# Sum of squared differences by row: another order of the last pieces, and a closing without barriers

## The chip, the cores and the metric

One core of one Trainium2 chip. Times are device microseconds of a whole execution; the span is the stretch that the profile covers, from the first issued load to the last instruction. The program runs on one core, so there is no second die to compare with; all the runs reported here were classed fast, and the granted clock was 1.00 in each. A semaphore is a counter by which one engine waits for another; at a barrier every engine waits for all the others.

## The reference

```python
batch, dim = 1024, 4096            # x and y, float32, standard normal
def reference(x, y, axis):         # axis = -1
    return np.sum((x - y) ** 2, axis=axis).astype(np.float32)
```

33.5 MB are read and 4 KB written.

## The kernel before

Each of the 128 partitions holds 8 rows of 4096 columns side by side, so that a load is a run of columns over all partitions: 32768 columns of x and as many of y. The buffers hold 6 rows; rows 6 and 7 go where rows 0 and 1 lay. VectorE subtracts in place, ScalarE squares and sums each piece of a row into one column, and pieces of one row are added up at the end. A few columns of row 3 ("late") are held back and loaded near the end, so that there is work that needs no new load of x.

```python
xw = [16384, 8192, 3072, 2688, 1312, 768, 352]   # widths of the loads of x
yw = [15648, 8192, 3072, 2688, 1312, 768]        # of y; the first stops 736 short of row 3's end
late, last = 736, 352
...
ys += [(cut, cut + late), (N - last, N)]         # row 3's end, then row 7's last 352 columns
...
for j, (c0, c1) in enumerate(ys):
    final, tail = j == len(ys) - 1, j == len(ys) - 2
    ...
        sub(*piece)                              # VectorE
        if final:                                # row 7: VectorE squares its last piece itself
            nc.vector.wait_ge(acts, squared[row_parts[r][-2]])
            nc.vector.tensor_reduce(out=head, in_=parts_of(r, len(row_parts[r]) - 1), ...)
            ...
            nc.vector.tensor_tensor_reduce(..., scalar=head, accum_out=results[:, r : r + 1])
            continue
        square(*piece, where[piece])             # ScalarE
        if tail:                                 # row 3: ScalarE adds its two parts
            nc.scalar.activation(out=results[:, r : r + 1], in_=b, func=Identity, bias=a)
...
nc.sync.wait_ge(sums, n["sums"])
nc.sync.wait_ge(acts, n["acts"])
nc.sync.dma_start(out=ov, in_=results).then_inc(stored, 16)
nc.sync.wait_ge(stored, 16)
prog.close()                                     # moves all of this ahead of the entry block's branch
```

The work is put into the program's entry block. Behind it come the branch and what leaving the tile context emits: a barrier of all engines, the clearing of the semaphores by GpSimd, a second barrier.

## Time and profile before

| | before |
|---|---|
| time, median of 3 runs | 86.06 us (86.02 to 86.1) |
| profiled run: time, span | 85.87, 84.1 us |
| last load landed | 80.30 |
| store issued | 81.71 |
| store landed | 83.1 |

In a group's line the columns are: source line, engine, operation, output and input, count, busy time and mean, then the idle time of that engine ahead of them and what ended it. In a timeline they are start, duration, engine, line, operation. In a line of an instruction's records come the count, the durations (least, median, greatest, in ns) and when the first and the last started. "Readout" below is the short instruction behind a square that writes out its sum (ACTIVATION_READ_ACCUMULATOR on ScalarE, DVE_READ_ACCUMULATOR2_ANT on VectorE). The lines of the kernel before stand in the prediction.

### The profile page before, as it was taken

What the parts mean: (1) busy time and instruction counts of PE and PEld (TensorE: products, weight loads), DVE (VectorE), ACT (ScalarE), POOL (GpSimd) and SP (SyncE); (2) the same over time, 40 slices, a digit from 0 to 9 for tenths busy, and PEclk for the clock granted to TensorE, in tenths of its full rate; (3) what the DMA queues carried; (4) which work ended last, traced back from release to release, by engine and by line L of the source; (5) the groups of instructions that cost most, each with busy time, mean ns of one, the idle gap of its engine ahead of it and who ended that gap; (6) DMA issues with size and microseconds to landing.
All of it is one profiled execution on the core that took longest, in us unless ns stands there. A gap on an engine that the chain in (4) does not pass through costs nothing.

```text
span 84.1 us, 110 instructions
## 1 busy us (share of the span) xinstructions
DVE 36.3 (43%) x17; ACT 31.6 (38%) x26; POOL 0.2 (0%) x4
## 2 busy tenths in 40 slices
DVE  0000000000000000000899999990699999199870
ACT  4200000000000000000007979799505979997980
POOL 0000000000000000000000000000000000000000
DMA  9479999992999999995899979996999999999900
GB/s 499 187 312 499 499 499 499 499 436 92 447 476 476 476 476 476 476 476 249 358 390 499 499 327 421 499 452 296 438 421 438 424 424 425 400 424 412 363 0 2
DMA packets 2304, 33.56 MB, mean 399 GB/s; under 512 B 384, under 2 KB 640, under 8 KB 1280
## 3 DMA queue, kind: packets, MB, share of 16 engines
q1 hardware_dynamic: 2304, 33.56, 94.1%
HBM read 33.55 MB, written 0.00 MB: 399 GB/s over the span
## 4 chain that ended last, share of the span: by engine, by line
DMA 71%; DVE 14%; ACT 10%; SPq 1%; issue 0%
DMA Y<-in_y_dram 71%; DVE X L172 14%; ACT X L178 10%; SPq L114 1%; ACT results L219 0%
## 5 line engine op out<-in xcount | busy, mean ns | idle before, releaser
L172 DVE TENSOR_TENSOR X<-X,Y 128x4096 f32<-128x4096 f32 (+8 forms) x13 | 35.6, 2781 | 45.2 <-DMA Y<-in_y_dram 45.1
L178 ACT ACTIVATE X<-X 128x4096 f32<-128x4096 f32 (+7 forms) x12 | 29.4, 2449 | 48.7 <-DVE X L172 48.7
L178 ACT ACTIVATION_READ_ACCUMULATOR X<-X 128x1 f32 x12 | 2.2, 186 | 0.0
L178 ACT ACT_TABLE_LOAD x1 | 1.3, 1283 | 1.3 <-PEq L264 1.3
L202 DVE CUSTOM_DVE_ANT_0 Y<-X,head 128x352 f32<-128x352 f32 x1 | 0.6, 583 | 0.1
L219 ACT ACTIVATE results<-parts 128x1 f32<-128x1 f32 x1 | 0.3, 294 | 0.0
L196 DVE TENSOR_REDUCE head<-parts 128x1 f32<-128x3 f32 x1 | 0.1, 150 | 0.0
L235 DVE TENSOR_REDUCE results<-parts 128x1 f32<-128x2 f32 x1 | 0.1, 147 | 0.0
L264 POOL MEMSET const-bfloat16-1.0<- 128x1 bf16 x1 | 0.1, 102 | 0.0
L264 POOL MEMSET const-uint8-127<- 128x1 uint8 x1 | 0.1, 102 | 0.0
L264 POOL MEMSET const-float32-0.0<- 128x1 f32 x1 | 0.1, 99 | 0.2 <-issue 0.2
L264 POOL MEMSET const-float32-1.0<- 128x1 f32 x1 | 0.1, 99 | 0.0
L202 DVE DVE_READ_ACCUMULATOR2_ANT results<- 128x1 f32 x1 | 0.1, 81 | 0.0
## 6 DMA issues: line engine op xcount, KB each, us to landing
Y<-in_y_dram SPq DMA_DIRECT2D x1, 7824.0 KB, 39.8
X<-in_x_dram SPq DMA_DIRECT2D x1, 4096.0 KB, 48.6
Y<-in_y_dram SPq DMA_DIRECT2D x1, 4096.0 KB, 58.0
X<-in_x_dram SPq DMA_DIRECT2D x1, 1536.0 KB, 14.9
Y<-in_y_dram SPq DMA_DIRECT2D x1, 1536.0 KB, 18.2
X<-in_x_dram SPq DMA_DIRECT2D x1, 1344.0 KB, 17.5
Y<-in_y_dram SPq DMA_DIRECT2D x1, 1344.0 KB, 20.4
X<-in_x_dram SPq DMA_DIRECT2D x1, 656.0 KB, 21.5
```

What stands on the lines that cost most here:

```text
L114: nc.sync.dma_start(out=dst[:, home(c0, c1)], in_=src[:, c0:c1]).then_inc(sem, 16)
L172: nc.vector.tensor_sub(out=a, in0=a, in1=Y[:, home(c0, c1)]).then_inc(diffs, 1)
L178: nc.scalar.activation(out=a, in_=a, func=Square, accum_out=acc).then_inc(acts, 1)
L196: nc.vector.tensor_reduce(out=head, in_=parts_of(r, len(row_parts[r]) - 1), axis=mybir.AxisListType.X, op=add).then_inc(sums, 1)
L202: nc.vector.tensor_tensor_reduce(out=Y[:, home(*piece)], in0=X[:, home(*piece)], in1=X[:, home(*piece)], scale=1.0, scalar=head, op0=mult, ...
L219: nc.scalar.activation(out=results[:, r : r + 1], in_=b, func=Identity, bias=a).then_inc(acts, 1)
L235: nc.vector.tensor_reduce(out=results[:, r : r + 1], in_=parts_of(r, len(row_parts[r])), axis=mybir.AxisListType.X, op=add,).then_inc(sums, 1)
L264: nc = _bacc.Bacc("TRN2", target_bir_lowering=False, num_devices=1)
```

## The change

Two things are changed together. The tail: other widths; row 3's end becomes the very last piece and is squared by VectorE, which adds the rest of the row as a scalar operand; row 7 is squared by ScalarE alone and summed by a VectorE reduce behind all else. The Identity on ScalarE and the first reduce go. The closing: the tile context is closed and compiled while it is still empty, so its barriers come at the start; at the end GpSimd alone waits for the store and clears the semaphores.

```diff
+        tc.close()
+        tc.compile()
 ...
+    def close(self, sem, value):
+        self.nc.gpsimd.wait_ge(sem, value)
+        self.nc.clear_and_free_semaphores(self.sems)
 ...
-    xw = [16384, 8192, 3072, 2688, 1312, 768, 352]
-    yw = [15648, 8192, 3072, 2688, 1312, 768]
-    late, last = 736, 352
+    xw = [16384, 8192, 5568, 1824, 512, 288]
+    yw = [16224, 8192, 2656, 2912, 928, 896, 512]
+    late, last = 160, 288
 ...
-    ys += [(cut, cut + late), (N - last, N)]
+    ys += [(N - last, N), (cut, cut + late)]
 ...
             if final:
-                nc.vector.wait_ge(acts, squared[row_parts[r][-2]])
-                nc.vector.tensor_reduce(out=head, ...)
 ...
-                    scalar=head,
+                    scalar=parts_of(r, 1),
 ...
-            if tail:
-                nc.scalar.activation(out=results[:, r : r + 1], in_=b, func=Identity, bias=a)
 ...
+    complete(7)                      # VectorE: wait for ScalarE, reduce row 7's five parts
     nc.sync.wait_ge(sums, n["sums"])
-    nc.sync.wait_ge(acts, n["acts"])
     nc.sync.dma_start(out=ov, in_=results).then_inc(stored, 16)
-    nc.sync.wait_ge(stored, 16)
-    prog.close()
+    prog.close(stored, 16)
```

## The prediction

> **What bounds the kernel now.** I read the page first, then the chain of waits in order of time, then the timeline of the last microseconds, and last the records of the program's closing line.
>
> The page of the kernel before, its head and the two widest groups:
>
> ```profile
> span 84.1 us, 110 instructions
> DVE 36.3 (43%) x17; ACT 31.6 (38%) x26; POOL 0.2 (0%) x4
> HBM read 33.55 MB, written 0.00 MB: 399 GB/s over the span
> DMA 71%; DVE 14%; ACT 10%; SPq 1%; issue 0%
> L172 DVE TENSOR_TENSOR X<-X,Y 128x4096 f32<-128x4096 f32 (+8 forms) x13 | 35.6, 2781 | 45.2 <-DMA Y<-in_y_dram 45.1
> ```
>
> No engine is busy half of the span. VectorE idles 45.2 us, nearly all on loads of y. 33.55 MB in about 80 us is the kernel; what can be saved is what follows the last byte, as the change reads the same bytes. The stretch from 59.65 (y's second load has landed) to 73.47 shows DMA share 1.00 and 420 to 426 GB/s in the view by windows: in steady state one column of one operand (128 x 4 B = 512 B) takes 512 / 426,000 = 1.20 ns.
>
> The chain of waits in order of time, its end:
>
> ```profile
> 53.11 20.36 DMA Y<-in_y_dram
> 73.47 0.02 issue
> 73.49 3.04 DVE X L172 x2
> 76.53 0.02 issue
> 76.56 4.75 ACT X L178 x8
> 81.31 0.02 issue
> 81.33 0.29 ACT results L219
> ```
>
> The last loads arrive one by one (issue plus time to landing, from the DMA list): y up to column 27648 at 66.98, up to 30336 at 73.47, to 31648 at 76.61, to 32416 at 78.49, row 3's 736 columns at 79.37, the last 352 at 61.30 + 19.0 = 80.30. The timeline:
>
> ```profile
> 79.53 0.83 ACT L178 ACTIVATE X<-X 128x768 f32<-128x768 f32 x1
> 80.26 0.19 ACT L178 ACTIVATION_READ_ACCUMULATOR X<-X 128x1 f32 x1
> 80.33 0.53 DVE L172 TENSOR_TENSOR X<-X,Y 128x352 f32<-128x352 f32 x1
> 80.39 0.82 ACT L178 ACTIVATE X<-X 128x736 f32<-128x736 f32 x1
> 80.77 0.15 DVE L196 TENSOR_REDUCE head<-parts 128x1 f32<-128x3 f32 x1
> 81.00 0.58 DVE L202 CUSTOM_DVE_ANT_0 Y<-X,head 128x352 f32<-128x352 f32 x1
> 81.11 0.18 ACT L178 ACTIVATION_READ_ACCUMULATOR X<-X 128x1 f32 x1
> 81.33 0.29 ACT L219 ACTIVATE results<-parts 128x1 f32<-128x1 f32 x1
> 81.52 0.08 DVE L202 DVE_READ_ACCUMULATOR2_ANT results<- 128x1 f32 x1
> 81.71 0.35 SPq L245 DMA_DIRECT2D out_dram<-results  x1
> ```
>
> From the last landing to the store's issue pass 1.41 us. Two paths end together: VectorE at 81.60 (352 columns subtracted, reduced, squared) and ScalarE at 81.62 (736 columns squared, the Identity that adds row 3's halves). The chain names ScalarE, by 0.02 us. The store lands 1.4 us after its issue, at 83.1. What follows, from the records of the closing line:
>
> ```profile
> L278 POOLq EVENT_SEMAPHORE  x4: 17/17/17, 83.4 to 84.0; - x4
> L278 SPq COMPARE_BRANCH  x1: 33/33/33, 83.1 to 83.1; - x1
> L278 POOLq EVENT_SEMAPHORE_RANGE_CLEAR  x1: 138/138/138, 83.7 to 83.7; - x1
> ```
>
> So SyncE wakes at 83.1 and branches; a barrier of all engines forms at 83.5, GpSimd clears all semaphores in one 138 ns instruction at 83.7, a second barrier ends at 84.0. That is nearly 1 us with no work in it.
>
> **What the Trainium skill says.** "ScalarE: Activation LUTs", section "What ACT_TABLE_LOAD costs", gives an ACTIVATE with immediate scale and bias 186 ns + 0.833 ns per column, and about 93 ns more for a pointer operand. The trace agrees: 768 columns took 827 ns (826 by the formula), 4096 took 3617 (3598), and the Identity, with its bias pointer, 294 ns on one column. "VectorE: DVE Perf Modes", section "Mode 2×_2P", has fp32 tensor_tensor held at 1x; the trace's subtractions (527 ns at 352 columns, 4421 at 4096) lie on 161 + 1.04 N. "DMA: Bandwidth & Descriptors", section "Anatomy of one DMA", puts most of a small DMA's fixed 2 us into the wait for the write's receipt; here the 4 KB store took 1.4 us, and the change leaves it. "Runtime: NRT & Kernel Launch", section "The launch sequence", lists work around the kernel that no program removes; here the profiled run measured 85.87 us against a span of 84.1, so 1.8 us lie outside of the span, and I keep them.
>
> **The change, part by part.** First the start. The tile context's own drains and barriers now come before the work. The first two loads still go into the entry block ahead of them, so the DMA starts as before. The other loads wait for perhaps 1 us more of barriers and a branch; but the second load of y occupies the queue until 40.19, so nothing is lost.
>
> The middle. Third load of x: 5568 columns instead of 3072, which needs rows 0 and 1 freed, so it is issued after row 1 is squared (52.74 before, some 53.3 now, as y's first load is 576 columns longer at about 1.05 ns, 0.6 us) instead of at 48.41. y's second load fills the queue to 59.65 + 0.6 = 60.25, so this too is hidden. The load count stays 15.
>
> The tail. All bytes still end at about 80.30. I place the other landings by counting columns of both operands against the before kernel's landings, at 1.20 ns each: y to 30144 ends with column 60128 against 59936 at 73.47, so 73.70; y to 31072: 62880 against 62560 at 76.61, so 76.99; to 31968: 63776 against 64096 at 78.49, so 78.11; to 32480: 64800 against 64832 at 79.37, so 79.33; to 32768: 65376 against 65536 at 80.30, so 80.10; row 3's last 160 at 80.30.
>
> VectorE, by 161 + 1.04 N, successors starting 0.07 before the predecessor's recorded end: 1440 columns from 73.72; 1472 from 75.31 to 77.00; 928 from 77.01 to 78.14; row 6's reduce (0.15) and 896 to 79.34; 512 to 80.05; 288 from 80.12 to 80.58; 160 to 80.84; the square-and-add of 160 (583 - 192 x 1.04 = 383 ns) from 80.92 to 81.30. VectorE alone would be done with row 3 at 81.3.
>
> ScalarE, by 186 + 0.833 N: 1472 can start at 77.03 and takes 1.41; then 928 (0.96), 896 (0.93), 512 (0.61), 288 (0.43). The sum is 4.34 and each operand is ready before its turn, so it runs through to 81.37, and with the accumulator's read (0.09 past the end, as in 81.11 + 0.18 against 80.39 + 0.82) to 81.46. Then VectorE's reduce of row 7's five parts: 0.04 + 0.15, to 81.65; the store's issue 0.09 later, 81.74. Before: 81.71. So the tail gains nothing, by my sum: the Identity (0.29) goes, but row 7 now has all of its pieces on ScalarE, where 352 columns were on VectorE, and a reduce stands behind it. I take 0 with ±0.2.
>
> The end. Store issued at 81.7, landed at 83.1. GpSimd waits for it: about 0.05 to wake, perhaps its drain (0.09) and a gap of 0.1 ahead of the clear as before, 0.14 for the clear: 83.35 to 83.4 against 84.07. One range clear is assumed, as the semaphores are allocated in one go. Gain: 0.7.
>
> Sum: start 0, middle 0, tail 0.0, end -0.7. 86.06 - 0.7 = 85.36; I put 85.3, since the other four engines are long finished when GpSimd ends, which may shorten the runtime's closing a little.
>
> **The rivals.** (1) The tail is worth its full intent: VectorE sets the end, row 7's reduce starts at 81.3, the store at 81.5: 0.2 to 0.3 more, 85.0. For it: VectorE is at rest from 81.3 in my sum. Against: ScalarE's 4.34 us after 77.03. It takes the third y load landing 0.2 us earlier than I counted. (2) The clearing is not on the path, or GpSimd clears 19 semaphores one by one: 19 x 138 ns = 2.6 us, 88 us. Against: before, one range clear did it. (3) The runtime's closing takes the place of the barrier removed: the 0.7 us stay, 86.0. For it: 1.8 us outside of the span, of which the profile shows nothing. Against: before, the engines' barrier came ahead of these, not within. (4) The late issue of the third x load starves the queue at 60. Issues took up to 3.16 us each when many loads were outstanding; a bubble would move the last landing one for one. Against: 53.3 is 7 us ahead of need.
>
> **Range and chances.** Tail ±0.2, end ±0.15, runs ±0.1 (86.02 to 86.1), and the rivals: 84.9 to 85.7. Faster by over 2% means under 84.34, 1 us below my sum, more than rival 1 and a shorter closing can give: 0.05. Slower needs rival 2: 0.01. Within 2%: 0.94.
>
> **What would show it.** The last load should land at 80.3 ± 0.2. ScalarE should run without idle time from the 1472-column square to the 288-column one, and the reduce of five parts should wait for ScalarE, not for VectorE's own square of 160. If it starts right after the latter, the tail step is wrong. Behind the store's landing there should be one range clear on GpSimd and no event semaphores of other engines; the span should end 0.2 to 0.3 us after the landing, at 83.4. If the span shrinks by 0.7 and the time doesn't, rival 3 holds. A gap in the DMA row near 60 us is rival 4.

## The result, and the profile after

| | before | after |
|---|---|---|
| time, median of 4 runs each | 86.04 us | 85.32 us (85.2 to 85.4) |
| ratio, 95% interval | | 0.9916 (0.9899 to 0.9934) |
| profiled run: time, span | 85.87, 84.1 | 85.35, 83.5 |
| last load landed | 80.30 | 65.07 + 15.4 = 80.47 |
| store issued | 81.71 | 81.82 |
| store landed | 83.1 | 83.2 |

A ratio here is the mean time of one kernel's runs over that of the other's of the same rounds, so it is not quite the ratio of the medians beside it. The change saves 0.7 us, under 1%: by the rule of 2% the two count as the same.

The page after, its head:

```profile
span 83.5 us, 109 instructions
DVE 36.3 (44%) x18; ACT 31.7 (38%) x27; POOL 0.2 (0%) x4
HBM read 33.55 MB, written 0.00 MB: 402 GB/s over the span
```

The same bytes, and busy times within 0.1 us. The chain of waits, its end:

```profile
54.11 16.24 DMA Y<-in_y_dram
70.35 0.02 issue
70.37 2.94 DVE X L165
73.31 0.02 issue
73.33 8.28 ACT X L171 x14
81.61 0.02 issue
81.64 0.16 DVE results L178
```

ScalarE's part of the last stretch has grown from 4.75 us and 8 records to 8.28 us and 14: from 73.33 on it goes from one square to the next. The chain now leaves the loads at 70.35, 10 us before the last one lands: the last landing no longer stands on it. The last of the timeline after:

```profile
81.02 0.39 DVE L199 CUSTOM_DVE_ANT_0 Y<-X,parts 128x160 f32<-128x160 f32 x1
81.08 0.43 ACT L171 ACTIVATE X<-X 128x288 f32<-128x288 f32 x1
81.33 0.08 DVE L199 DVE_READ_ACCUMULATOR2_ANT results<- 128x1 f32 x1
81.41 0.19 ACT L171 ACTIVATION_READ_ACCUMULATOR X<-X 128x1 f32 x1
81.64 0.16 DVE L178 TENSOR_REDUCE results<-parts 128x1 f32<-128x5 f32 x1 [0.23 <-ACT X L171]
81.82 0.35 SPq L226 DMA_DIRECT2D out_dram<-results  x1
```

VectorE is done with row 3 at 81.41 and stands idle for 0.23 us until ScalarE has read out row 7's last sum at 81.60. Only then does the reduce of five parts run. From the last landing to the store's issue pass 81.82 - 80.47 = 1.35 us; before it was 1.41. In the changed kernel this is a distance between two paths and no path itself, as ScalarE's chain sets the end. What remains behind the store's landing, the records of the closing line after:

```profile
L46 POOLq DRAIN  x1: 88/88/88, 83.3 to 83.3; - x1
L46 POOLq EVENT_SEMAPHORE_RANGE_CLEAR  x1: 138/138/138, 83.4 to 83.4; - x1
```

One drain and one clear, both on GpSimd. From the store's issue to the end of the span it was 84.1 - 81.71 = 2.4 us and is 83.5 - 81.82 = 1.7: this is where the time went.

### The profile page after: what moved, and what is told of

Read it like the earlier page. It is cut to its first block, busy times and chain, and to the rows that moved or that the text cites. A ratio compares the mean times of both kernels' runs of the same rounds, so it can differ in the third digit from the quotient of the medians.

```text
span 83.5 us, 109 instructions
## 1 busy us (share of the span) xinstructions
DVE 36.3 (44%) x18; ACT 31.7 (38%) x27; POOL 0.2 (0%) x4
## 4 chain that ended last, share of the span: by engine, by line
DMA 68%; ACT 14%; DVE 14%; SPq 1%; issue 0%
DMA Y<-in_y_dram 68%; ACT X L171 14%; DVE X L165 14%; SPq L108 1%; DVE results L178 0%; SPq L215 0%
## 5 line engine op out<-in xcount | busy, mean ns | idle before, releaser
L165 DVE TENSOR_TENSOR X<-X,Y 128x4096 f32<-128x4096 f32 (+9 forms) x14 | 35.8, 2593 | 45.2 <-DMA Y<-in_y_dram 45.1
L171 ACT ACTIVATE X<-X 128x4096 f32<-128x4096 f32 (+8 forms) x13 | 29.7, 2287 | 48.0 <-DVE X L165 48.0
## 6 DMA issues: line engine op xcount, KB each, us to landing
Y<-in_y_dram SPq DMA_DIRECT2D x1, 4096.0 KB, 58.3
```

Source lines behind the costliest of these rows:

```text
L165: nc.vector.tensor_sub(out=a, in0=a, in1=Y[:, home(c0, c1)]).then_inc(diffs, 1)
L171: nc.scalar.activation(out=a, in_=a, func=Square, accum_out=acc).then_inc(acts, 1)
```

## The experiments

Theory: the closing alone makes the gain, as its barriers lay behind the store's landing; the tail gains nothing to speak of, as ScalarE takes the place of the path removed. Rivals: the tail gains too; the early closing of the context gains by itself; what the closing saves comes back outside of the span.

Twelve runs were made, in three sets of four, each set beside the kernel before. Means and medians below are of the set's runs. The second set holds no run of the changed kernel, so its kernels can be compared with that one only by the ratios to before.

**The yardstick, first set.** The changed kernel once more, no edit.

> The changed kernel once more, as the yardstick of this set on the same chip. Both theories: ratio 0.991 to 0.992 of before (85.3 against 86.05 us).

Measured: 85.2 us median against 86.01, ratio 0.9905 (0.9886 to 0.9925). Profiled: last load at 64.88 + 15.4 = 80.28, store issued 81.58, span 83.3. The difference from the first profile is in the loads: y's first landed at 40.81 instead of 41.12. One profile places the last landing only to about 0.2 us.

**The closing alone.** Before's widths and tail, with the changed closing.

```diff
+        tc.close()
+        tc.compile()
 ...
-    nc.sync.wait_ge(stored, 16)
-    prog.close()
+    prog.close(stored, 16)
```

> Before's data plan and tail; only the context closed at once and GpSimd waiting and clearing. Theory (the gain is the closing alone, the tail is worth 0): 85.3 to 85.45 us, ratio 0.991 to 0.993, store issued at 81.7, span 83.4. Rival (both parts gain): 85.6 to 85.8. Rival (the runtime's closing swallows the end and the tail made the gain): 86.0.

Measured: 85.4 us, ratio 0.9925 (0.9907 to 0.9942). Profiled: store issued at 81.85 (expected 81.7), 1.38 us behind a last landing at 61.47 + 19.0 = 80.47; span 83.6, so the closing takes 1.75 us. In means the closing saves 86.042 - 85.398 = 0.64 us. The theory's figure for the closing, 0.7, holds; both rivals (a smaller share for the closing, or none) fall.

**The tail alone.** The new widths and order, with before's closing.

```diff
-    prog.close(stored, 16)
+    nc.sync.wait_ge(stored, 16)
+    prog.close()
```

(and the context closed on leaving, as before)

> The new widths, row 3's end last, row 7 reduced behind it, but before's closing with its barriers. Theory: 86.0 to 86.2 us, store issued at 81.7 to 81.85, span 84.1 to 84.2. Rival (the tail gains): 85.6 to 85.8.

Measured: 85.81 us, ratio 0.9977 (0.9958 to 0.9996); in means 86.042 - 85.837 = 0.2 us. The median is 0.19 us below the theory's range and 0.01 above the rival's, and the store's issue was 0.1 earlier than expected: the tail does gain a little, with an interval of 0.03 to 0.36 us, and that it is worth nothing is not borne out. The two parts add up: 0.64 + 0.20 = 0.84 against 0.81 for the yardstick. In the trace, VectorE's reduce waits 0.24 us for ScalarE here too, and the store is issued at 81.60, 1.34 us behind the last landing at 64.86 + 15.4 = 80.26.

**Barriers put back, the context still closed early.**

```diff
-        self.nc.gpsimd.wait_ge(sem, value)
+        self.nc.sync.wait_ge(sem, value)
+        self.nc.all_engine_barrier()
         self.nc.clear_and_free_semaphores(self.sems)
+        self.nc.all_engine_barrier()
```

> The changed kernel with its early-closed context, but at the end SyncE waits for the store, a barrier of all engines, the clear, and a second barrier. Theory (what is saved is the two barriers, not the early closing): 85.95 to 86.2 us, span 84.1 to 84.2. Rival (closing the context early saves by itself, a branch and instruction fetch at the end): 85.5 to 85.8.

Measured: 85.72 us, ratio 0.9964 (0.9946 to 0.9982). That is above the yardstick by 85.732 - 85.230 = 0.50 us and below the tail with before's closing by 85.837 - 85.732 = 0.1, which the intervals don't separate. It misses my expected range by 0.23 us and lies inside the rival's. Both ranges took the tail to be worth nothing; with the 0.2 us that the run before gave it, the theory's would be 85.75 to 86.0 and the rival's 85.3 to 85.6, and the measured time lies between them, next to the theory's. So the barriers are most of it, and not all. The records of the line of its second barrier, in part:

```profile
L48 POOLq EVENT_SEMAPHORE  x2: 17/17/17, 83.7 to 83.8; - x2
L48 SPq EVENT_SEMAPHORE  x1: 17/17/17, 83.8 to 83.8; - x1
```

And those of the line of its clear, which stands between the two barriers:

```profile
L47 POOLq DRAIN  x1: 88/88/88, 83.3 to 83.3; - x1
L47 POOLq EVENT_SEMAPHORE_RANGE_CLEAR  x1: 138/138/138, 83.4 to 83.4; - x1
```

The clear starts at 83.4 here with the store issued at 81.64, and in the changed kernel at 83.4 with the store issued at 81.82: the first barrier delays it by some 0.2 us, and the second one adds 0.3 us behind it. So barriers are 0.5 of the 0.64 us; the rest, 0.1, would be the branch that no longer stands between the store and the closing, which is argued from the trace and not shown by the times.

**The drain ahead of the clear left out.**

```diff
-        self.nc.clear_and_free_semaphores(self.sems)
+        ids = sorted(s.num for s in self.sems)
+        self.nc.gpsimd.sem_clear(range(ids[0], ids[-1] + 1))
```

> The changed kernel, its clear written out as one range clear over the same 19 semaphores, without the 88 ns drain that stands ahead of it. Theory (GpSimd's wait, drain and clear lie in series behind the store's landing): 0.1 to 0.2 us less than the changed kernel, ratio to before 0.988 to 0.9895. Rival (the drain is hidden in the wait): no change, 0.9905.

Measured: 85.17 us, ratio 0.9907 (0.9879 to 0.9936), with single runs at 85.48 and 85.7: inconclusive.

**ScalarE's last square left out** (wrong in row 7).

```diff
+            if piece == row_parts[7][-1]:
+                continue
             square(*piece, where[piece])
 ...
-                in_=parts_of(r, len(row_parts[r])),
+                in_=parts_of(r, m),          # m is one less for row 7
```

> The changed kernel with the square of row 7's last 288 columns left out and its reduce over four parts (wrong in row 7 on purpose). Theory (ScalarE ends the tail, 0.23 us behind VectorE): the reduce follows VectorE's own square at once, store 0.2 to 0.25 earlier after the last landing, ratio to before about 0.988. Rival (the last landing and VectorE set the end): no change, 0.9905.

Measured: 84.9 us, ratio 0.9866 (0.9841 to 0.9891). The timeline, its end:

```profile
81.15 0.08 DVE L200 DVE_READ_ACCUMULATOR2_ANT results<- 128x1 f32 x1
81.15 0.15 DVE L179 TENSOR_REDUCE results<-parts 128x1 f32<-128x4 f32 x1
81.33 0.35 SPq L229 DMA_DIRECT2D out_dram<-results  x1
```

The reduce follows VectorE's own square with no idle time, and the store is issued 81.33 - (64.89 + 15.4) = 1.04 us behind the last landing, not 1.30 to 1.37. So in the changed kernel ScalarE sets the end of the tail, and VectorE's path ends 0.3 us sooner. The rival, that the last landing and VectorE set it, falls.

**More and smaller pieces.** If ScalarE's queue from the 1472 columns on is at fault, pieces that shrink evenly should empty it.

```diff
-    xw = [16384, 8192, 5568, 1824, 512, 288]
-    yw = [16224, 8192, 2656, 2912, 928, 896, 512]
-    late, last = 160, 288
+    xw = [16384, 8192, 4864, 1344, 896, 544, 320, 224]
+    yw = [16256, 8192, 2720, 2144, 1344, 896, 544, 320]
+    late, last = 128, 224
```

> The changed kernel with row 6 and 7 in seven shrinking pairs of loads (2720, 2144, 1344, 896, 544, 320, 224) and 128 columns of row 3 last; 17 loads instead of 15. Theory (ScalarE's queue from the 1472 columns on is what sets the end): ScalarE is no longer behind, store issued 0.2 us earlier, less some 0.05 for two loads: ratio to before 0.988 to 0.9895. Rival (the end follows the last landing, and two more loads delay it): 0.9905 to 0.992.

Measured: 85.13 us median, ratio 0.9903 (0.9878 to 0.9928): no gain that can be told from the yardstick. The widths make 18 loads, not the 17 that I wrote. The trace shows both halves of why: ScalarE's last readout ends at 81.36, before VectorE's own square (81.43), and the store follows the last landing by 0.99 us; but the last load now lands at 69.59 + 11.0 = 80.59, and at 69.78 + 10.9 = 80.68 in the next kernel, which has the same loads, where the three profiles of the changed kernel have 80.28, 80.29 and 80.47. The theory holds for ScalarE and fails for the cost of three more loads, as I had put two at some 0.05. The delay is not the scatter of the start: from the landing of y's first load to that of the last one pass 39.60 and 39.66 us in these two kernels, and 39.34 to 39.47 in the changed kernel. Whether the number of the loads or their sizes cause it was not tested.

**Both.**

```diff
-        self.nc.clear_and_free_semaphores(self.sems)
+        self.nc.gpsimd.sem_clear(range(ids[0], ids[-1] + 1))
 ...
-    xw = [16384, 8192, 5568, 1824, 512, 288]
+    xw = [16384, 8192, 4864, 1344, 896, 544, 320, 224]     # and yw, late, last as above
```

> The seven pairs and the clear without a drain together. Theory: the two gains add, 84.8 to 84.95 us, ratio to before 0.986 to 0.988. Rival: no better than the better of the two alone.

Measured: 85.11 us, ratio 0.9888 (0.9863 to 0.9912). Short of what was expected, and not separated from either alone: inconclusive.

**The yardstick, third set.** No edit.

> The changed kernel as the yardstick of this set. Ratio to before 0.9905, 85.2 to 85.3 us.

Measured: 85.27 us median against 86.1, ratio 0.9909 (0.9893 to 0.9926).

**Without the drain, again.** The same edit as above.

> The kernel without the drain again, now beside the changed kernel in one set, as its interval was too wide. Theory: 0.1 us under the changed kernel (span 0.1 to 0.15 shorter behind the store's issue). Rival: equal.

Measured: 85.1 us, ratio 0.9883 (0.9869 to 0.9898), in means 85.288 - 85.093 = 0.2 us under the yardstick of the set. The records of its clear:

```profile
L48 POOLq EVENT_SEMAPHORE_RANGE_CLEAR  x1: 138/138/138, 83.2 to 83.2; - x1
```

From the store's issue to the end of the span it is 83.3 - 81.71 = 1.59 us (1.56 in the first run of this kernel), where the changed kernel has 1.68, 1.72 and 1.64 in its three profiles. So the trace gives the drain 0.1 us; the intervals of the ratios in this set still overlap a little (0.9869 to 0.9898 against 0.9893 to 0.9926), and the set before showed nothing. I take 0.1 as the better figure.

**Sixteen loads.** Six shrinking pieces, the first two under one load of x.

```diff
-    xw = [16384, 8192, 5568, 1824, 512, 288]
-    yw = [16224, 8192, 2656, 2912, 928, 896, 512]
-    late, last = 160, 288
+    xw = [16384, 8192, 5280, 1344, 800, 480, 288]
+    yw = [16256, 8192, 2560, 2720, 1344, 800, 480]
+    late, last = 128, 288
```

> The changed kernel with rows 6 and 7 in six shrinking pieces (2560, 2720, 1344, 800, 480, 288), the first two under one load of x, 128 columns of row 3 last: 16 loads, one more than before. Theory: ScalarE no longer behind VectorE at the end, one load costs 0.05 us: 0.1 to 0.2 us under the changed kernel. Rival (each load costs as much as the queue of ScalarE gives back, as with 18 loads): equal.

Measured: 85.08 us, ratio 0.9881 (0.9867 to 0.9895), in means 0.22 us under the yardstick. The end of the timeline:

```profile
81.19 0.19 ACT L171 ACTIVATION_READ_ACCUMULATOR X<-X 128x1 f32 x1
81.23 0.08 DVE L199 DVE_READ_ACCUMULATOR2_ANT results<- 128x1 f32 x1
81.41 0.16 DVE L178 TENSOR_REDUCE results<-parts 128x1 f32<-128x5 f32 x1
81.59 0.35 SPq L226 DMA_DIRECT2D out_dram<-results  x1
```

ScalarE ends at 81.38 and VectorE at 81.31, 0.07 us apart instead of 0.19; the store follows the last landing (67.29 + 13.1 = 80.39) by 1.20 us. From y's first landing to the last one pass 39.33 us (39.34 in the kernel below, with the same loads), so this one load more cost nothing that shows. The interval still touches that of the yardstick.

**Sixteen loads and no drain.**

```diff
-        self.nc.clear_and_free_semaphores(self.sems)
+        self.nc.gpsimd.sem_clear(range(ids[0], ids[-1] + 1))
 ...
-    xw = [16384, 8192, 5568, 1824, 512, 288]
+    xw = [16384, 8192, 5280, 1344, 800, 480, 288]          # and yw, late, last as above
```

> The sixteen loads and the clear without its drain together. Theory: 84.9 to 85.05 us, 0.2 to 0.3 under the changed kernel of this set. Rival: within 0.1 of it.

Measured: 84.95 us, ratio 0.9867 (0.9852 to 0.9882), which lies wholly below the yardstick's interval: in means 85.288 - 84.940 = 0.35 us faster than the changed kernel of the same set, and 1.14 us faster than the kernel before. It is the fastest correct version here.

## Why the prediction was right or wrong

**Start and middle, 0: right.** The other loads were issued from 1.91 us on instead of 1.26, and the third load of x at 53.73 instead of 48.41, and neither shows: the loads behind y's second follow it without a pause: it landed at 2.29 + 58.3 = 60.59, and the next 5568 + 2656 columns at 70.35, which is 1.19 ns a column. The 2912 behind them landed at 73.84. By column count I had 73.70 for that; y's first load landed at 41.12 and in the next profile at 40.81, where I had 40.8. Nor is there a gap near 60 us, the sign of rival 4: from 41.12 to 60.60 the DMA share was 1.00. Some slips in the prediction change nothing: of the "two widest groups" its first lines show one; 40.19 is the landing of y's first load, not of its second; and by its own rule the 896 columns end on VectorE at 79.24, not 79.34, but the next piece waits for a landing at 79.33 anyway.

**The tail, 0 ± 0.2: right in its mechanism, at the edge of its size.** ScalarE ran through without idle time, the reduce waited for it and not for VectorE (0.23 us), and leaving out ScalarE's last square freed VectorE's path. ScalarE's readout ended at 81.60 against 81.46 by the sum, VectorE's square at 81.41 against 81.30, and the landings that these two waited for were later by about as much: the 2912 columns by 0.14 us, the last load by 0.17. The tail alone then measured 0.2 us faster, not 0. Of that the traces show about 0.05 behind the last landing: 1.41 and 1.38 us from landing to store with the old tail, 1.25 to 1.40, about 1.33 in the mean, over seven profiles with the new one. The rest would be an earlier last landing. A count that leaves out the scatter of the start gives less: from the landing of y's first load to the store's issue pass 41.52 and 41.53 us with the old tail and 40.69 to 40.77 over the same seven profiles with the new one. Of these 0.8 us, 0.69 are the 576 columns that the new first load already holds, at 1.20 ns each; so my estimate for the tail is 0.1 us, within the interval of 0.03 to 0.36 from the times. The profile that I read of before was of a quick execution, 85.87 us against a median of 86.04, so that typical landings of before lie some 0.15 later than the 80.30 that I counted from; but with only two traces of the old tail this is argued, not shown. So the forecast of 0 had the right engine at the end and a size too small by 0.1 to 0.2. Whether the new widths themselves bring the bytes sooner stays open.

**The end, -0.7: right.** From the store's issue to the end of the span it saved 2.4 - 1.7 = 0.7 us; in the time, alone, it measured 0.64. One range clear did all, 0.3 us after the store's landing as in the sum, with the drain and the wake-up in it. Before's clear of one instruction was the right guide against rival 2.

**The rivals.** Rival 1 (the tail's full worth, 0.2 to 0.3 more) wanted ScalarE out of the way; it was not, though its size is close to what the tail gave by another route. Rival 3 (the saving comes back outside) falls but for a small part: the closing alone shortened the time by 0.64 us and the mean span by 0.69. In one detail the prediction erred: I rounded 85.36 to 85.3 because the part outside of the span might shrink. It grew, from 1.79 us in the mean of before to 1.85 of the changed kernel (11 and 6 runs of the first set). This goes with the closing: in the means, kernels that keep the barriers have 1.78 to 1.80 and those without 1.81 to 1.86 (each span is recorded to 0.1 us). The guess had the wrong sign, and that 85.3 came within 0.02 us of the measured 85.32 is luck: what the tail gained made up for it.

## What to carry to other kernels

Everything behind the last store's landing counts nearly in full: here two all-engine barriers cost half a microsecond, and one engine that waits for the store and clears the semaphores in one instruction is enough. When work is moved from one engine's tail to another's, add up the queue of the engine that receives it, piece by piece, from the last point at which it must wait: here ScalarE worked without a pause from 73.33 to 81.60 and ended 0.19 us behind VectorE, so that dropping an instruction of 0.3 us gained only 0.1 to 0.2. Finer pieces empty such a queue, but each further load may delay the last byte: one load more went with a gain here, three more did not.

## What the Trainium skill lacked or had wrong

- "Runtime: NRT & Kernel Launch", section "The launch sequence", lists preamble and postamble at some 9 to 15 us. In the times of these runs, all that lies outside of the span is 1.79 us (kernel before) to 1.85 us (changed kernel), so most of that list is not in this metric, or doesn't occur; the runs don't tell which. Nor does it say what ending on one engine alone does to that part: it grew by 0.06 us.
- No page gives the cost of clearing a range of semaphores: 138 ns for 19 of them, 158 ns for 22, in one instruction, and 88 ns for the drain ahead of it.
- No page gives the cost of an all-engine barrier that a program has at its own end: putting the two back cost 0.50 us.
- "DMA: Bandwidth & Descriptors", section "Anatomy of one DMA", has a fixed cost of about 2 us for the path from GpSimd. The 4 KB store from SyncE took 1.4 us from issue to landing in every profile here; for that path the page gives a latency to the first byte, but no time from issue to landing.
